# A fused matmul, GELU and matmul: the first load of b in two column halves

## The chip, the cores and the metric

The kernel runs on one core of a Trainium2 chip. The metric is the device time of one execution in microseconds, as the median of several runs; lower is better. A profile of one execution belongs to it: its span runs from the first to the last instruction and is a little shorter than the device time.

## What is computed

All inputs are float32: a is 1024 x 1024, b is 1024 x 2048, c is 2048 x 1024.

```python
h = np.matmul(a, b)
h = 0.5 * h * (1 + np.tanh(np.sqrt(2 / np.pi) * (h + 0.044715 * h ** 3)))
return np.matmul(h, c).astype(np.float32)
```

## The kernel before

The kernel keeps everything on the chip between the two products. It makes aᵀ in bf16 (`aT`), multiplies with b to get the transposed hidden matrix, applies GELU into `hT`, and multiplies with c. The order of all instructions is written out by hand (a manual schedule), so each engine runs its instructions in the order of the program text, and a wait at the head of an engine's order holds up everything behind it.

The columns of b are handled in stages. The first 512 columns (four tiles of 128, t = 0 to 3) are multiplied in the plain way while the inputs still arrive; this is the stage of the change. The next 512 and then the last 1024 columns, and the whole second product, go through `seven`, which computes a 2 x 2 block product with seven block multiplications instead of eight (Winograd's form of Strassen's method), with sums of blocks made on VectorE (DVE), and copies on ScalarE (ACT).

**The first loads.** a and the first 512 columns of b come over SyncE's queue (SP) as float32 into staging tiles, `sta` and `stb`. One load of a, `load_a(h, q)` (L70), brings 512 rows (half h) and 256 columns (quarter q) in runs of 1 KB. One load of b, `load_b(q)` (L74), brings two slabs of 128 rows (k = 2q and 2q+1) and 512 columns, in runs of 2 KB. Each is 512 KB. They are issued in the order a(0,0), b(0), a(1,0), then for q = 1 to 3: a(0,q), b(q), a(1,q). All other loads (the rest of b, and c) go over GpSimd's queue (POOL) and are cast to bf16 on the way; they start only when the copy into `gate` (L84) has seen a(1,2) land.

**The first stage.** `stir` (L116) runs matmuls on a tile of zeros, to warm up TensorE; they are part of TensorE's fixed order and wait for no load. `cast_a` (L99 on ACT, L101 on DVE) turns a staged quarter of a into bf16 (`ab`), `turn` transposes it on TensorE in two groups of four (L132) with a DVE copy from the accumulator bank into `aT` after each group (L133). `cast_b` (L139, on ACT) turns one slab of b into bf16 (`b1`), `block` and `mm1` (L105) are the matmuls. The beginning of TensorE's order is: four warm-ups of 256 columns; a group of transposes of a(0,0); a warm-up of 256; the second group; a warm-up of 128; then

```python
    cast_b(0, 2)
    cast_b(1)
    ab = cast_a(1, 0, nc.vector, nc.scalar)
    block(0, range(4), (0,))
    block(0, range(2), (1,))
    tn = turn(1, 0, 7, ab)
    next(tn)
```

`cast_b(0, 2)` casts slab 0 in two instructions of 256 columns each: the first holds the columns that tiles t = 0 and 1 need, the second those of t = 2 and 3. `cast_b(1)` casts slab 1 in one instruction of 512. The matmuls of `block` follow, four with slab 0 and two with slab 1, and then the transposes of a(1,0), whose cast is shared between DVE and ACT.

**The stores.** In the second product `done2` stores a finished tile of the output over SyncE's queue (`store`, L436). For the upper left block, (i, l) = (0, 0), each of the tiles j = 0, 1 and 2 is stored in two halves of 256 columns; other tiles go out in one store of 512 columns. The buffers that they are stored from (`o`) are four in rotation. The tile j = 3 of that block is computed last of all, in two halves (L380 to L383).

Of the kernel before, what the change touches and what calls it, by code (L numbers as in the profile page):

```python
# [19 lines left out]
def kernel(ctx, tc, a, b, c, out):  # L20
    nc = tc.nc
# [3 lines left out]
    H = 512  # L25
# [4 lines left out]
    bv = b.rearrange("(kt p) n -> p kt n", p=128)  # L30
# [9 lines left out]
    def slot(tag, shape, dt, name):  # L40
        return big.tile(shape, dt, name=name, tag=tag)
# [4 lines left out]
    def pieces(tag, bufs, shape, dt, name):  # L46
        return small.tile(shape, dt, name=name, tag=tag, bufs=bufs)
# [18 lines left out]
    stb = slot("x0", [128, KT, H], F32, "stb")  # L66
    sta = [slot(f"x{i}", [128, 2, 2, 4, 256], F32, "sta") for i in (1, 3)]

    def load_a(h, q):
        nc.sync.dma_start(out=sta[q // 2][:, h, q % 2],  # L70
                          in_=av[:, 4 * h:4 * h + 4, ds(q * 256, 256)])

    def load_b(q):
        nc.sync.dma_start(out=stb[:, 2 * q:2 * q + 2], in_=bv[:, 2 * q:2 * q + 2, 0:H])  # L74

    load_a(0, 0)
    load_b(0)
    load_a(1, 0)
    for q in range(1, 4):
        load_a(0, q)  # L80
        load_b(q)
        load_a(1, q)
# [7 lines left out]
    for n in range(2):  # L90
        for k in range(0, KT, 4):
            nc.gpsimd.dma_start(out=b2[:, k:k + 4, ts(n, H)],
                                in_=bv[:, k:k + 4, ds(1024 + n * H, H)])
# [341 lines left out]
    def store(mt, q0, w, ot, eng=None):  # L435
        (eng or nc.sync).dma_start(out=out[ts(mt, 128), ds(q0, w)], in_=ot)  # L436

    def done2(i, l, j, p):
        if (i, l) == (1, 0):
            ot = pieces("o", 4, [128, H], F32, "ot")  # L440
            nc.vector.tensor_copy(ot, p)
            p = ot
        n = 2 if (i, l) == (0, 0) else 1
        for q in range(n):
            r = ds(q * (H // n), H // n)
            store(4 * i + j, l * H + q * (H // n), H // n, p[:, r])

    def between2(n):
# [12 lines left out]
        elif n == "P73":  # L461
            two.t4(two.t[1], 4)

    seven(two, done2, between2)


# [28 lines left out]
```

## Time and profile before

The time before is 118.21 us, the median of three runs (118.2 to 118.34). The profiled execution had a span of 116.2 us and a mean granted TensorE clock of 0.999.

| | busy us | share of the span |
|---|---|---|
| TensorE matmul (PE) | 111.7 | 96% |
| TensorE weight load (PEld) | 76.9 | 66% |
| VectorE (DVE) | 90.3 | 78% |
| ScalarE (ACT) | 59.3 | 51% |
| GpSimd (POOL) | 11.0 | 9% |

| SyncE's loads and stores | count | KB each | median us from issue to landing |
|---|---|---|---|
| a into `sta` | 8 | 512 | 8.4 |
| b into `stb` | 4 | 512 | 8.0 |
| output, whole tiles | 12 | 256 | 2.1 |
| output, halves | 8 | 128 | 2.0 |

How to read the profile: PE and PEld are the two sides of TensorE, whose weight loads run beside the matmuls. Matmuls are pipelined, so the records of neighbours overlap, and a busy PE need not be PE at its peak; the spacing of starts tells the pace. L74 means line 74 of the kernel. "idle before, releaser" names what ended an engine's idle time. The chain of work is followed back from the last instruction: at each step to what released it. A DMA instruction's own record covers its issue on the engine's queue only; the transfer is seen in the DMA views and in what waits for it.

### The profile page before, as it was taken

The numbers are of one execution on the slowest core, as the hardware profiler recorded it, in microseconds if no ns is written. First come the engines' busy times: TensorE is split into PE (matmuls) and PEld (weight loads), VectorE is DVE, ScalarE is ACT, GpSimd is POOL, SyncE is SP. The second block draws the span as 40 slices with busy tenths as digits, with TensorE's granted clock in tenths as the row PEclk, the third lists the DMA queues.
The fourth block names the chain that finished last, engine by engine and source line by source line (L and its number), as shares of the span: only waits on it lengthen the run. The fifth ranks groups of instructions, "written<-read, shape, count | busy, mean of one in ns | idle before, by whom it ended". The sixth has DMA issues, their size and how long they took to land.

```text
span 116.2 us, 1478 instructions
## 1 busy us (share of the span) xinstructions
PE 111.7 (96%) x540; PEld 76.9 (66%) x540; DVE 90.3 (78%) x107; ACT 59.3 (51%) x99; POOL 11.0 (9%) x21
## 2 busy tenths in 40 slices
PE   5999999999999999999999999999999999999980
PEld 4655555545777447888885444588888888888860
DVE  0336666889998999844699999999999986954770
ACT  5067668989269998066699329600034982000000
POOL 2000049623322000000000000000000000000000
PEclk9999999999999999999999999999999999999999
DMA  2999999999999999998000000070000002014993
GB/s 83 298 356 393 395 395 321 206 206 206 206 208 213 211 213 211 213 209 164 4 0 0 0 6 0 7 264 0 0 0 0 0 0 96 0 69 171 370 364 109
DMA packets 13542, 17.91 MB, mean 154 GB/s; under 512 B 736, under 2 KB 8928, under 8 KB 13536
## 3 DMA queue, kind: packets, MB, share of 16 engines
q0 software_dynamic: 5344, 7.34, 35.6%
q1 hardware_dynamic: 8192, 10.49, 25.2%
q8 instruction: 4, 0.07, 0.2%
q14 instruction: 2, 0.02, 0.0%
HBM read 20.97 MB, written 4.19 MB: 217 GB/s over the span
## 4 chain that ended last, share of the span: by engine, by line
PE 96%; DVE 1%; issue 0%
PE ps L197 76%; PE ps L105 12%; PE ps L116 4%; PE pt L132 4%; DVE aT L133 0%; DVE ot L382 0%; DVE warm L50 0%
## 5 line engine op out<-in xcount | busy, mean ns | idle before, releaser
L197 PE MATMUL ps<-x,s 128*128 128x512 f32 x128 | 29.6, 391 | 0.0
L197 PEld LDWEIGHTS ps<-x,s 128*128 128x128 f32 x128 | 24.0, 188 | 5.1
L197 PE MATMUL ps<-x,x 128*128 128x512 f32 x96 | 22.9, 394 | 0.0
L197 PEld LDWEIGHTS ps<-x,x 128*128 128x128 f32 x96 | 18.0, 188 | 3.9
L105 PE MATMUL ps<-aT,b 128*128 128x512 bf16 x64 | 16.3, 379 | 0.0
L305 ACT ACTIVATE v<-ps 128x512 f32<-128x512 f32 x10 | 6.0, 598 | 19.4 <-PE ps L197 19.4
L197 PE MATMUL ps<-c_sb,hT 128*128 128x512 bf16 (+1 forms) x72 | 14.2, 356 | 0.0
L197 PE MATMUL ps<-x 128*128 128x512 f32 x56 | 13.2, 393 | 0.0
L197 PEld LDWEIGHTS ps<-x 128*128 128x128 f32 x56 | 10.2, 188 | 2.7 <-ACT u L305 0.4
L133 DVE COPY aT<-pt 128x512 bf16<-128x512 bf16 x16 | 6.8, 424 | 6.4 <-PE pt L132 6.4
L197 PEld LDWEIGHTS <-hT 128*128 128x128 bf16 x72 | 6.9, 98 | 7.0 <-issue 0.5
L109 ACT ACTIVATE hT<-ot 128x512 bf16<-128x512 f32 x18 | 10.5, 625 | 1.5 <-DVE ot L310 1.3
L310 DVE TENSOR_TENSOR ot<-ps,v 128x512 f32<-128x512 f32 x10 | 6.7, 688 | 5.2 <-DMA out_dram<-ot 3.8
L197 PE MATMUL ps<-aT,b 128*128 128x512 bf16 x48 | 10.7, 379 | 0.0
L310 DVE TENSOR_TENSOR ot<-ps,u 128x512 f32<-128x512 f32 x10 | 6.7, 689 | 5.1 <-ACT u L305 5.1
L155 DVE TENSOR_TENSOR x<-c_sb 128x1024 fp32r<-128x1024 bf16 x8 | 9.2, 1221 | 0.0
L132 PEld LDWEIGHTS <-ab 128*128 128x128 bf16 x64 | 4.9, 102 | 5.5 <-DVE ab L101 1.9
L197 PEld LDWEIGHTS <-b 128*128 128x128 bf16 x48 | 4.6, 97 | 5.7 <-issue 0.3
L105 PEld LDWEIGHTS <-b 128*128 128x128 bf16 x64 | 5.5, 98 | 4.1 <-ACT b L139 0.5
L99 ACT ACTIVATE ab<-sta 128x512 bf16<-128x512 f32 x10 | 6.0, 625 | 3.3 <-DMA sta<-in_a_dram 3.3
L305 ACT ACTIVATE u<-ps 128x512 f32<-128x512 f32 x10 | 5.8, 596 | 3.4 <-PE ps L197 3.2
L109 ACT ACTIVATE hT<-ps 128x512 bf16<-128x512 f32 x14 | 7.3, 596 | 0.4 <-PE ps L105 0.3
(39 smaller groups left out, 115.6 us busy)
## 6 DMA issues: line engine op xcount, KB each, us to landing
sta<-in_a_dram SPq DMA_DIRECT2D x8, 512.0 KB, 8.4
c_sb<-in_c_dram POOLq DMA_DIRECT2D x8, 512.0 KB, 19.9
b<-in_b_dram POOLq DMA_DIRECT2D x6, 512.0 KB, 11.5
out_dram<-ot SPq DMA_DIRECT2D x12, 256.0 KB, 2.1
stb<-in_b_dram SPq DMA_DIRECT2D x4, 512.0 KB, 8.0
out_dram<-ot SPq DMA_DIRECT2D x8, 128.0 KB, 2.0
```

The source lines that it names most:

```text
L99: nc.scalar.activation(dst, src, AF.Copy)
L105: nc.tensor.matmul(p, b1[:, k, ts(t, 128)], aT[:, h, k], start=(k == 0), stop=(k == KT - 1))
L109: nc.scalar.activation(hT[h][:, t], p, AF.Gelu_apprx_tanh)
L116: nc.tensor.matmul(ps[0, 3][:, 0:w], warm[:, 0:128], warm[:, 0:w], start=True, stop=True, skip_group_check=True)
L132: nc.tensor.transpose(pt[:, n, ts(m, 128)], ab[:, m, ts(n, 128)], ident)
L133: nc.vector.tensor_copy(aT[:, h, 2 * q + n], pt[:, n])
L155: nc.vector.tensor_tensor(out=dst[:, r], in0=x[:, r], in1=y[:, r], op=op)
L197: nc.tensor.matmul(p[:, ds(c0, w)], l[:, k, ts(j, 128)], r[:, k, ds(c0, w)], start=(start and k == 0), stop=(k == self.kt - 1), skip_group ...
L305: nc.scalar.activation(st, p, AF.Copy)
L310: nc.vector.tensor_tensor(out=ot, in0=p, in1=st, op=ADD)
```

## The change

b's first load is split by columns: `load_b(0, 2)` issues one load for columns 0 to 255 of slabs 0 and 1 and one for columns 256 to 511, each of 256 KB and in runs of 1 KB. The other three loads of b stay whole. It is for the first half-cast of `cast_b(0, 2)`, which then waits for the first of the two loads instead of the whole. The second half-cast waits for the second one.

With the second edit the tile j = 2 of the upper left output block is stored whole instead of in two halves. SyncE's queue then carries 13 loads and 19 stores instead of 12 and 20, and the stores behind that tile keep their number in the queue's order.

```diff
-    def load_b(q):
-        nc.sync.dma_start(out=stb[:, 2 * q:2 * q + 2], in_=bv[:, 2 * q:2 * q + 2, 0:H])
+    def load_b(q, n=1):
+        for i in range(n):
+            r = ds(i * (H // n), H // n)
+            nc.sync.dma_start(out=stb[:, 2 * q:2 * q + 2, r], in_=bv[:, 2 * q:2 * q + 2, r])
 
     load_a(0, 0)
-    load_b(0)
+    load_b(0, 2)
     load_a(1, 0)
...
-        n = 2 if (i, l) == (0, 0) else 1
+        n = 2 if (i, l) == (0, 0) and j < 2 else 1
         for q in range(n):
             r = ds(q * (H // n), H // n)
             store(4 * i + j, l * H + q * (H // n), H // n, p[:, r])
```

## The prediction

> **What bounds the kernel now.** I read the page first: the engines, and the chain that ended last.
>
> ```profile
> PE   111.7 (96%) x540; PEld 76.9 (66%) x540; DVE 90.3 (78%) x107; ACT 59.3 (51%) x99; POOL 11.0 (9%) x21
> ...
> PE 96%; DVE 1%; issue 0%
> ```
>
> TensorE carries 96% of the chain; busy time alone would not prove a bound, but the chain says that almost every step was released by the one before it on the same engine. Then the chain in order of time, at the place where b's first load is used (start, length, what):
>
> ```profile
> 1.19 3.78 PE ps L116 x8
> 4.97 0.01 issue
> 4.99 0.61 PE pt L132 x4
> 5.59 0.96 PE ps L116 x2
> 6.55 0.35 PE pt L132 x4
> 6.90 0.28 PE ps L116 x2
> 7.18 1.32 PE ps L105 x6
> 8.50 0.35 PE pt L132 x4
> 8.85 0.02 issue
> 8.88 0.44 DVE aT L133
> ```
>
> From 1.19 to 8.85 us TensorE runs without a hole: the warm-up matmuls of `stir` (L116), eight transposes (L132), then the first six matmuls that need b (L105). The warm-ups stand in TensorE's own order and wait for no load. After this there is one DVE step of 0.44 us and then TensorE to 112.98 us. The timeline of the same stretch (start, length, engine, line, what, idle before and its releaser) shows who waits for which load:
>
> ```profile
> 6.56 1.24 ACT L139 ACTIVATE b<-stb 128x256 bf16<-128x256 f32 x3 [4.33 <-DMA stb<-in_b_dram]
> ...
> 7.03 1.47 PE L105 MATMUL ps<-aT,b 128*128 128x512 bf16 x6
> ...
> 7.33 0.24 PEld L105 LDWEIGHTS <-b 128*128 128x128 bf16 x2 [0.19 <-ACT b L139]
> ...
> 7.86 0.15 PEld L105 LDWEIGHTS <-b 128*128 128x128 bf16 x2 [0.28 <-ACT b L139]
> ...
> 7.96 0.43 DVE L101 CAST ab<-sta 128x512 bf16<-128x512 f32 x1 [0.59 <-DMA sta<-in_a_dram]
> ...
> 8.44 0.23 PEld L132 LDWEIGHTS <-ab 128*128 128x128 bf16 x4 [0.43 <-DVE ab L101]
> ```
>
> ACT idles 4.33 us for b's first load; that looks like the prize. But the six matmuls take 1.47 us, that is five spacings and a last one of 0.38: (1.47 - 0.38) / 5 = 0.218 us each. Elsewhere three take 0.81 us: (0.81 - 0.38) / 2 = 0.215. So the weight loads that waited 0.19 and 0.28 us for ACT cost the matmuls about 5 x 0.003 = 0.015 us. The next thing does cost: six matmuls at 0.217 from 7.03 are issued by 8.33, and the transposes start only at 8.44, when DVE's cast of the second a load (7.96 to 8.39) is done. The **second load of a**, `load_a(1, 0)`, is what binds, by 0.11 us, and it stands in the queue right behind the load that is changed.
>
> Last, the windows of the DMA (start:end, length, five engines' busy time, clock, DMA share, GB/s):
>
> ```profile
> 4.00:4.50 0.50, 0.50 (x3) 0.25 (x1) 0.26 (x1) 0.00 (x0) 0.00 (x0) 1.00 0.99 262
> 4.50:5.00 0.50, 0.48 (x3) 0.02 (x2) 0.43 (x1) 0.00 (x0) 0.00 (x0) 1.00 0.86 184
> ...
> 9.00:9.50 0.50, 0.41 (x5) 0.14 (x3) 0.30 (x1) 0.06 (x1) 0.00 (x0) 1.00 1.05 410
> 10.50:11.00 0.50, 0.50 (x6) 0.27 (x4) 0.50 (x2) 0.46 (x2) 0.00 (x0) 1.00 1.08 383
> ```
>
> By adding up the bytes of all such windows I can say which load is moving: 0.52 MB (the first a load) are through at 3.65 us, 1.05 MB (plus b's first) at 5.6. So the first two lines are b's first load, with the DMA engines 86 to 99% busy and yet slow; the third is b's second load, in the same 2 KB runs and fast; the fourth is a, in 1 KB runs.
>
> **What the Trainium skill says.** "DMA: Bandwidth & Descriptors", section "Queues, rings and completion order": each DMA engine takes one queue's descriptors in ring order, and a load is split over the 16 engines. So the order of issue on SyncE is the order of landing; the trace agrees (landings used at 4.24, 6.56, 7.96, 9.44 us in the order of issue). The same page, "Why small descriptors are slow (HBM only)": each packet has an overhead of some 3 beats of 32 bytes, so 1 KB is 35 beats for 32 and 2 KB 67 for 64; an estimate from this is 4.5% less rate at 1 KB. The trace has 383 (1 KB) against 410 and 397 GB/s (2 KB; the 397 is the window from 13.0 to 13.5 us), 5%; I use the trace.
>
> **The change part by part.**
>
> *First half earlier.* b's first 256 columns (0.26 MB) are through when 0.79 MB are: by the windows at 4.45 us, and with the lag of about 0.6 to 0.9 us between bytes and use (3.65 to 4.24 for a, 5.6 to 6.56 for b) ACT can cast them near 5.3 instead of 6.56. The second half-cast still waits for the whole half megabyte, so it starts near 6.6 to 6.65 where it started at 6.88, and the cast of k=1 ends near 7.7 instead of 7.80. Queued behind them on ACT is half of the second a cast, which waits for its own load at 7.96 anyway. What TensorE gets is the 0.015 us above: it reaches its first b matmul at 7.03 because of the warm-ups. **Worth: 0 to 0.015 us, and the latter vanishes in the 0.11 us wait behind it.**
>
> *1 KB runs.* At a's rate the 0.524 MB take 0.524/0.383 = 1.369 us; at 404 GB/s (the mean of 410 and 397, the windows of b's second load and its third) they take 1.298: **+0.07 us**. The second load adds one completion packet per engine; at most one 1 KB packet's 0.04 us, I take 0.02. Together the next load is **0.09 us** later.
>
> *One more issue on SyncE.* About 0.5 us each at the start (1.23 to 1.73). The issue of `load_a(1, 0)` moves from 1.78 to about 2.25. Its bytes begin to move at 5.6 us, so this costs 0; the work that hides it is the queue of earlier bytes. Behind it all later issues move by at most 0.5 us, with some four loads in the queue ahead: 0.
>
> *Stores.* For one tile (j=2) two stores of 128 KB become one of 256 KB at 75 to 77 us. The DMA is otherwise idle there (28% share from 72 to 80), SyncE has no other work, and the next writer of such a buffer comes at 94.4: 0.
>
> *Sum.* The second a load, binding by 0.11 us, is used at 7.96 + 0.09 = 8.05, and every step behind it moves by as much: DVE's cast, the transposes, and, as all later loads are 0.09 later too, the next rounds, which have no room (at 12.03 and 16.07 ACT waits for the DMA while DVE has just come free). TensorE's chain has no slack from 8.44 to 112.98 to take it up. 118.21 + 0.09 = **118.3 us**, 0.08% more, which can't be told from no change.
>
> **The rivals.** *Slow start grows* (slower). From 4.0 to 5.0 us 109 packets of 2 KB took (0.99 + 0.86) x 0.5 x 16 = 14.8 us of engine time, 0.136 each, against 0.084 in the window from 9.0 (1.05 x 8 / 100). Some 180 packets were that slow: 180 x 0.052 / 16 = 0.6 us lost. I don't know why. If the loss is per packet, twice as many packets lose it twice: +0.6 on the +0.09, **118.9 us**. For it: the engines are busy, not starved, in that stretch. Against: b's first 70 packets ran at 404 GB/s with the same runs, and so did its second load.
>
> *Slow start eases* (a little faster). "DMA: Bandwidth & Descriptors", "Latency and other measured facts", tells of streams in lock-step that fall on the same memory channels (its pitches are far larger than the 8 KB here, and it calls the mechanism an inference). All 16 engines end the first a load within 0.5 us, so they start b in step; other runs may break that. Then the second a load comes up to 0.6 us sooner, but TensorE can use only 0.11 of it before its own matmuls bind at 8.33; afterwards DVE, which casts the third a pair right after a copy that ends at 12.04, sets the pace. **118.1 us** at best. For a gain over 0.24 us I find no idle time on TensorE that this change could reach.
>
> **How the numbers follow.** The plain sum 0.47 (118.3), slow start grows 0.29 (118.9), eases 0.24 (118.1). The first gives "within 0.2%" (118.0 to 118.45) nearly always, the second slower, the third mostly within, with a part faster because a bound of 0.11 read from one trace may be short. Faster 0.13, same 0.57, slower 0.30. The range runs from 117.95, a little under the best that I can work out, to 118.9, the full loss; the chance outside it is that a rival is larger than worked out.
>
> **What would show it.** In the new profile: the first half-cast near 5.3 with an idle time of some 3 us, the first L105 matmul still at 7.03, the cast at 7.96 moved to about 8.05 and the transposes at 8.44 to 8.5. If those transposes stand at 8.35 the start eased; at 9 it grew. It would be wrong if the first b matmul itself moves, for then the warm-ups don't set it, or if the times differ while the transposes stand still.

## The result, and the profile after

The changed kernel takes 119.58 us, the median of six runs (118.87 to 119.96), against 118.23 (118.2 to 118.43) for the kernel before beside it. The ratio is 1.0104, with a 95% interval of 1.0068 to 1.014: slower; the medians differ by 1.35 us. The kernel before repeats within 0.23 us here, the changed one within 1.1; but in the larger batches of the experiments the kernel before has outliers too (118.04 to 119.26 in 23 executions), so the spread by itself proves nothing. Five executions in the experiments (one each in runs 2, 3, 4, 7 and 18) were over 1.5% above the fastest of their kernel and are left out of the ratios; the profiles of runs 2 and 4 are of such executions. The profiled execution of the changed kernel is one of the two slowest of the six, with a span of 118.2 us where the one before had 116.2, so the sizes read from it are at the upper end.

First the chain that ended last, in order of time (start, length, what), in the changed kernel:

```profile
2.29 7.66 DMA sta<-in_a_dram
9.94 0.02 issue
9.97 0.44 DVE ab L103
10.41 0.05 issue
10.45 0.41 PE pt L134 x4
...
114.96 0.42 DVE ot L384
```

Before, TensorE's warm-ups, transposes and matmuls made up this part of the chain. Now one line stands in their place: the second load of a, issued at 2.29 and landed at 9.94. The transposes that it releases start at 10.45 where they started at 8.44, and the last step starts at 114.96 where it started at 113.00. The 2.0 us are there at the first of these points, and nothing later gives them back or adds to them.

The timeline of the same stretch (start, length, engine, line, what, idle before and releaser):

```profile
4.88 0.42 ACT L141 ACTIVATE b<-stb 128x256 bf16<-128x256 f32 x1 [2.65 <-DMA stb<-in_b_dram]
...
6.96 0.59 PE L107 MATMUL ps<-aT,b 128*128 128x512 bf16 x2
...
8.62 0.93 ACT L141 ACTIVATE b<-stb 128x256 bf16<-128x256 f32 x2 [3.32 <-DMA stb<-in_b_dram]
9.09 0.11 PEld L107 LDWEIGHTS <-b 128*128 128x128 bf16 x2 [2.03 <-ACT b L141]
9.09 1.12 PE L107 MATMUL ps<-aT,b 128*128 128x512 bf16 x4 [1.54 <-ACT b L141]
...
9.97 0.43 DVE L103 CAST ab<-sta 128x512 bf16<-128x512 f32 x1 [2.67 <-DMA sta<-in_a_dram]
```

The first half of b does what it was split for: its cast starts at 4.88, 1.68 us sooner. In this execution TensorE has no use for it, for its first b matmul stands behind the warm-ups, at 6.96. The second half, which the third and fourth matmuls need, is cast at 8.62 where it was 6.88, and TensorE stands idle for 1.54 us. Its granted clock stayed full from 6.59 us to the end of the work, and the mean granted clock is 0.996 or more in all six, so the loss is not a lower clock.

The windows of the DMA (start:end, length, five engines' busy time, clock, DMA share, GB/s) show the two halves and what follows:

```profile
3.50:4.00 0.50, 0.50 (x3) 0.41 (x2) 0.00 (x0) 0.00 (x0) 0.00 (x0) 1.00 1.10 387
4.00:4.50 0.50, 0.50 (x3) 0.25 (x1) 0.30 (x1) 0.00 (x0) 0.00 (x0) 1.00 1.20 301
4.50:5.00 0.50, 0.50 (x3) 0.05 (x2) 0.40 (x1) 0.12 (x1) 0.00 (x0) 1.00 0.62 143
5.00:5.50 0.50, 0.50 (x5) 0.50 (x6) 0.00 (x0) 0.30 (x1) 0.00 (x0) 1.00 0.70 158
5.50:6.00 0.50, 0.50 (x3) 0.41 (x3) 0.40 (x1) 0.00 (x0) 0.00 (x0) 1.00 0.77 170
```

The kernel before had 262 and 184 GB/s from 4.0 to 5.0 us, at shares of 0.99 and 0.86. Now the share falls to between 0.62 and 0.77: a good part of the DMA engines has nothing in flight, though the second half had been issued at 1.78 to 2.24 and the second a load from 2.29. That is one part of the loss. The other is that what is in flight moves slowly: at a share of 1.10 the engines moved 387 GB/s, so a share of 0.62 should move 218 and moved 143. The packets in the trace say how: of the 230 packets of 1 KB that start between 4.5 and 6.0 us the median takes 46 ns, but 20 take over 150 ns, up to 755, and these 20 hold 6.7 us of the 24 us that 16 engines have in this stretch. What they wait for no view shows.

The trace also holds the 16 times at which a DMA engine finished its part of a load, without the engine's number. A load counts as landed when the last one has. First and last, in us from the start:

```
                  a(0,0)       b(0), or its halves         a(1,0)
kernel before     3.87-4.21    5.58-6.54                   7.09-7.93
changed kernel    3.85-4.18    4.54-4.86  5.34-8.60        7.23-9.94
```

The first part of a(1,0) is done 0.14 us later than before, the last 2.01. In the first half the engines ended within 0.32 us of each other; in the second they come apart by 3.3 us, and the kernel waits for the last.

### The profile page after: what moved, and what is told of

Read it like the earlier page. It is cut to its first block, busy times and chain, and to the rows that moved or that the text cites. A ratio compares the mean times of both kernels' runs of the same rounds, so it can differ in the third digit from the quotient of the medians.

```text
span 118.2 us, 1472 instructions
## 1 busy us (share of the span) xinstructions
PE 111.6 (94%) x534; PEld 76.8 (65%) x540; DVE 90.2 (76%) x107; ACT 59.4 (50%) x99; POOL 11.0 (9%) x21
## 4 chain that ended last, share of the span: by engine, by line
PE 88%; DMA 6%; SPq 1%; DVE 1%; issue 1%
PE ps L199 74%; PE ps L107 10%; DMA sta<-in_a_dram 6%; PE pt L134 3%; SPq L76 1%; DVE ab L103 0%; SPq L70 0%; DVE aT L135 0%; DVE ot L384 0%
## 5 line engine op out<-in xcount | busy, mean ns | idle before, releaser
L141 ACT ACTIVATE b<-stb 128x512 bf16<-128x512 f32 (+1 forms) x9 | 4.8, 575 | 6.1 <-DMA stb<-in_b_dram 6.0
```

Source lines behind the costliest of these rows:

```text
L141: nc.scalar.activation(b1[:, k, r], stb[:, k, r], AF.Copy)
```

## The experiments

Each kernel is an edit of one of the two, and each comparison is with the kernel before on the same chip. In the measured lines "b" and "a(1,0)" are first and last engine as above; they come from one profiled execution each, the ratios from all that count. The edits are cut to the lines that matter.

**1. The load's split without the store's edit.**

```diff
-        n = 2 if (i, l) == (0, 0) and j < 2 else 1
+        n = 2 if (i, l) == (0, 0) else 1
```

> The split of b's first load alone; the stores as in the kernel before. In the changed kernel the two halves are fully landed at 4.86 and 8.60 us where the whole load landed at 6.54, and the second load of a at 9.94 where it was 7.93. All theories say that this comes from the load: about 119.6 us, TensorE's fifth b-tile wait of 1.5 us there again. If the stores had a part, this run is nearer to 118.2.

Measured: 119.95 us, ratio 1.0135 (1.0093 to 1.0177); halves 4.41-5.16 and 5.37-7.29, a(1,0) 7.53-8.79. The loss is there without the store's edit; the two intervals overlap, so that edit has no part that can be told.

**2. Two loads, but cut by slab, with 2 KB runs.**

```diff
+            w = 2 // n
+            r = slice(2 * q + i * w, 2 * q + i * w + w)
+            nc.sync.dma_start(out=stb[:, r], in_=bv[:, r, 0:H])
```

> b's first load also comes as two loads of 256 KB, but cut by slab (k = 0, k = 1), so both keep runs of 2 KB; stores as in the changed kernel. Theory R (the 1 KB runs of b, taken by all engines in step, are what is slow): 118.2 to 118.4 us, second a load landed by 8.1. Theory N (a second load in the opening burst of SyncE's issues is what is slow): about 119.6, second a load landed near 10.

Measured: 119.49 us, ratio 1.0086 (1.005 to 1.0122); b 4.90-6.46 and 5.54-8.66, a(1,0) 7.85-10.03. The interval overlaps that of the cut by columns, so theory R, short runs, doesn't explain this one. The landings are of the longest execution, 121.57 us, in which the first half was late as well, and are not used for sizes.

**3. One load with 1 KB runs.**

```diff
+        if q == 0:
+            o = o.rearrange("p k (n c) -> p (k n) c", n=2)
+            i = bv[:, 0:4, 0:256]
```

> One load of 512 KB for b's first, as before, but in 512 runs of 1 KB: it reads columns 0 to 255 of slabs 0 to 3 in place of columns 0 to 511 of slabs 0 and 1, so that part of the computation works on other numbers; sizes, waits and the stores are those of the kernel before. Theory R: 119 us or more, second a load landed at 9 or later. Theory N: 118.3 (the 0.07 us of shorter runs).

Measured: 118.2 us, ratio 0.9999 (0.9983 to 1.0015); b 5.24-5.68, a(1,0) 6.79-7.92. Twice as many packets in one load cost nothing. The windows from 4 us on:

```profile
4.00:4.50 0.50, 0.50 (x3) 0.24 (x1) 0.12 (x1) 0.00 (x0) 0.00 (x0) 1.00 1.09 389
4.50:5.00 0.50, 0.47 (x2) 0.00 (x0) 0.50 (x1) 0.00 (x0) 0.00 (x0) 1.00 1.05 373
5.00:5.50 0.50, 0.36 (x4) 0.37 (x5) 0.08 (x1) 0.00 (x0) 0.00 (x0) 1.00 0.77 236
5.50:6.00 0.50, 0.50 (x4) 0.48 (x2) 0.22 (x1) 0.30 (x1) 0.00 (x0) 1.00 0.94 281
```

b's load runs at full rate, which it did not in the kernel before, and the dip comes only afterwards, when the third load begins. So 1 KB runs are not the cause, and a whole load of them is even faster at this place than one of 2 KB runs.

**4. The second a load ahead of b.**

```diff
-    load_b(0)
     load_a(1, 0)
+    load_b(0)
```

> Kernel before with the issue order a(0,0), a(1,0), b(0) in place of a(0,0), b(0), a(1,0). It asks whether the slow stretch of the DMA (184 to 289 GB/s from 4 to 6 us in the kernel before) belongs to the time or to b's load. Theory T (the time): a(1,0), in flight from 3.7, is slow, 200 to 290 GB/s from 4 to 6, and b's first is fast. Theory R: a(1,0) runs at 385 and b's first load, from 5.1 us, is slow. b can be used only when its load has landed, near 7.5 (T or R), so TensorE starts on it some 0.6 us later and the time is 118.6 to 119.

Measured: 122.34 us, ratio 1.03 (1.0234 to 1.0366); a(1,0) 5.15-5.60, b, now third, 7.10-9.57. a(1,0) ran at 385 to 391 GB/s up to 4.5 us, so the slow stretch doesn't belong to the time: theory T falls. b was far slower than theory R said, and in third place slower than it had been in second; the time is far above the 118.6 to 119 that I expected. TensorE then sat idle for 3.3 us and came back at half its pace, with starts 0.40 to 0.43 us apart where 0.22 is usual: the granted clock was 0.50 from 8.84 to 15.67 us in this execution. That is why the time lost more than the landing.

**5 and 6. Later issues held back until the first a load has landed,** in the kernel before and in the changed one.

```diff
     load_a(1, 0)
+    nc.gpsimd.tensor_copy(sta[0][:, 0, 1, 0, 0:1], sta[0][:, 0, 0, 0, 0:1])
```

> Kernel before, with SyncE's issues paced: a one-column copy on GpSimd reads the first a load and writes into the destination of a(0,1), so SyncE issues that load and all later ones only when the first a load has landed (4.2 us) instead of from 2.3 us; three loads are queued until then. The column is overwritten by the load. Theory B (the slow stretch comes from the long run-ahead of issues in the opening): b's first load moves at 380 to 410 GB/s, lands near 5.5 instead of 6.54, the second a load near 7.0, and the time is 118.1 (0.1 us less, as TensorE's own order binds next). Theory M (memory or engine side, whatever is queued): slow stretch as before, second a load near 7.9, 118.2.

> The changed kernel with the same pacing (a(0,1) and later loads issued only after the first a load has landed). Theory B: the second half of b lands near 5.6 and the second a load near 7.1 instead of 8.60 and 9.94, the time 118.1 to 118.2. Theory M: again about 119.6, halves landing up to 3 us apart.

Measured: 120.34 us, ratio 1.0146 (1.0084 to 1.0208), and 120.23, 1.0174 (1.0139 to 1.0209). With the hold a(1,0) landed sooner in both (7.53 for 7.93; 8.48 for 9.94), but a(0,1), issued at 5.15 and 5.00, finished only at 8.46-10.73 and 8.79-10.58: the engines ran dry. In the kernel before so edited the issue of a(0,1) was over at 5.51, and yet from 6.5 to 7.5 us, as engines came free from a(1,0), the DMA share was 0.83 and 0.84, with 211 and 195 GB/s. Theory B is not confirmed, and the test was blunt, since it made a new hole. It shows that a load issued a full microsecond earlier can still leave engines without packets.

**7. b's first load taken from a.**

```diff
+        src = av if q == 0 else bv
+        nc.sync.dma_start(out=stb[:, 2 * q:2 * q + 2], in_=src[:, 2 * q:2 * q + 2, 0:H])
```

> Kernel before, but the first load into b's staging tile reads from a (row pitch 4 KB) in place of b (row pitch 8 KB), with the same 256 runs of 2 KB and the same waits; so part of the computation works on other numbers. Theory P (where b's rows lie in memory makes its first load slow): the load runs at 380 to 410 GB/s and lands near 5.5; 118.1. Theories B and M without P: slow stretch as before, landing near 6.5; 118.2.

Measured: 118.11 us, ratio 0.9986 (0.9967 to 1.0004); b's place 5.99-6.56, with 238 and 217 GB/s from 4 to 5 us. The slow stretch of the kernel before is there with rows of a too: theory P falls.

**8 and 9. Issues spaced by fills on GpSimd, about one per us,** in the kernel before and in the changed one. The later loads of b have a fill of `stb` ahead of them in the same way.

```diff
+    def paced_a(h, q):
+        nc.gpsimd.memset(sta[q // 2][:, h, q % 2], 0.0)
+        load_a(h, q)
```

> Kernel before; from the third load on, GpSimd first fills the destination of each load with zeros (about 1 us each, one after the other), and SyncE's load waits for it. So the loads are issued about one per us instead of one per half us, with no wait for data. The fills are overwritten. Theory B (issues that come in a burst are delivered to the DMA engines late and in pieces): b's first load lands near 5.5 instead of 6.54, the second a load near 7, all windows from 4 us on above 340 GB/s, time 118.1. Theory M (the slow stretch comes from the memory or the engines at a change of load): as before, 6.5, 7.9, 118.2.

> The changed kernel with the same spacing of issues from its fourth load on. Theory B: second half of b near 5.6, second a load near 7, 118.1 to 118.2. Theory M: halves of b landing up to 3 us apart, second a load near 9 to 10, 119.6.

Measured: 118.76 us, ratio 1.0041 (1.0026 to 1.0056), and 119.84, 1.0124 (1.0065 to 1.0183); b 5.28-6.69 and, with the split, 4.57-5.65 and 5.49-8.41; a(1,0) 7.42-8.05 and 7.74-9.81. Theory B falls: with the issues behind the halves spaced, the second half still lands at 8.41. The fills cost something of their own: beside them DVE's cast of a(1,0) took 1.19 us in the kernel before so edited where it had taken 0.43, so the two ratios are not the loads' alone.

**10 and 11. Another load of b split:** the second (fifth in the queue), and the last (eleventh).

```diff
-    load_b(0, 2)
+    load_b(0)
...
-        load_b(q)
+        load_b(q, 2 if q == 1 else 1)
```

> The changed kernel, but the load of b that is split is the second one (fifth in the queue) and the first stays whole. Theory B: one more issue in the opening burst, but behind b's first load and the second a load; those land as in the kernel before or a little later, time 118.2 to 118.8. A theory in which only the place right behind the first a load matters: 118.2 to 118.3.

> The changed kernel, but the split load of b is the last one (eleventh in the queue)[...]. Both theories: the split costs only its shorter runs, 118.2 to 118.3. If it costs about a microsecond here as well, the cost is in the split load itself and not in the opening.

Measured: 118.16 us, ratio 0.9986 (0.9972 to 1.0), and 118.25, 0.9996 (0.9987 to 1.0004). Free, in both places; a(1,0) landed at 7.91 and 8.11. Both kernels have the store's edit, so that is free too. Neither the split as such nor its 256 more packets costs anything that can be told, and an extra load that is issued as early as 3.41 us, fifth and sixth in the queue, doesn't either. The place of the split does.

**12. The same bytes as run 3, in two loads.** The second half comes from columns 0 to 255 of slabs 2 and 3.

```diff
+            c = ds(0, H // n) if q == 0 else r
+            k0 = 2 * q + (2 * i if q == 0 else 0)
+            nc.sync.dma_start(out=stb[:, 2 * q:2 * q + 2, r], in_=bv[:, k0:k0 + 2, c])
```

> The changed kernel, with the second half of b's first load taken from columns 0 to 255 of slabs 2 and 3 in place of columns 256 to 511 of slabs 0 and 1 (part of the computation works on other numbers). These are exactly the bytes, runs and order of the run with one load of 512 runs of 1 KB, which cost nothing (118.2), but in two loads. If the boundary between two loads is what stalls the DMA engines: 119.3 or more, halves landing 2 to 3 us apart. If the addresses are (columns 256 to 511, which no load before it has read): 118.2 to 118.4, no stall.

Measured: 118.59 us, ratio 1.0036 (1.0016 to 1.0057); halves 4.40-5.94 and 5.10-7.53, a(1,0) 7.24-8.93. Its windows beside those of run 3:

```profile
4.50:5.00 0.50, 0.14 (x1) 0.00 (x1) 0.45 (x1) 0.00 (x0) 0.00 (x0) 1.00 1.52 254
5.00:5.50 0.50, 0.50 (x5) 0.48 (x6) 0.06 (x1) 0.00 (x0) 0.00 (x0) 1.00 0.61 123
5.50:6.00 0.50, 0.47 (x4) 0.18 (x3) 0.36 (x1) 0.04 (x1) 0.00 (x0) 1.00 0.68 182
```

Where one load ran at 373 GB/s, two ran at 254, and 236 became 123. The bytes, the runs and their order are those of run 3, so the boundary costs here; but the times, 117.99 to 119.57 over 20 runs, are between the two expectations, and the interval stays below that of the changed kernel (1.0068 to 1.014). So where the second half is read from, or the chip that the run fell on, has a part in the size of the loss; which it is wasn't tested.

**13. The second half behind the second a load.**

```diff
-    load_b(0, 2)
+    load_b(0, 2, 0)
     load_a(1, 0)
+    load_b(0, 2, 1)
```

The third argument, added to `load_b`, picks the half.

> The changed kernel with the issue order a(0,0), first half of b, a(1,0), second half of b. If the third load in the queue stalls whatever it is, the second a load is slow now (landed after 8); if it is the second half of b itself, the second a load runs at 380 GB/s and lands near 6.3, and the second half behind it is slow. Time: TensorE's third b matmul needs the second half; with it landed near 7.1 118.2, with a stall 119 or more.

Measured: 120.06 us, ratio 1.0175 (1.0114 to 1.0235); first half 4.65-5.08, a(1,0) 6.20-7.32, second half 7.18-8.84. Both were slow: a(1,0), third, at 234 and 274 GB/s from 4.5 to 5.5 us, and the half behind it, fourth, at 207 to 252 from 6 to 8. So neither branch of the expectation holds alone: it isn't only the third load, and not only the half.

**14. b's first load issued first of all.**

```diff
-    load_a(0, 0)
     load_b(0)
+    load_a(0, 0)
```

> Kernel before with b's first load issued ahead of a's first, so order b(0), a(0,0), a(1,0). If the addresses of columns 256 to 511 or runs of 2 KB are slow on their first touch, b's load is slow although it is first (landed after 5). If it is the place in the queue, b's load lands near 4.2 and a later load stalls. TensorE's first transposes wait for a(0,0), now landed near 5.6 or later: 119 to 120 in both cases; the views of the DMA decide, not the time.

Measured: 121.37 us, ratio 1.0282 (1.0239 to 1.0324); b 4.49-5.35, a(0,0) 5.86-6.83, a(1,0) 7.21-8.19. Windows:

```profile
2.50:3.00 0.50, 0.50 (x2) 0.38 (x2) 0.00 (x0) 0.00 (x0) 0.00 (x0) 1.00 1.09 213
3.00:3.50 0.50, 0.50 (x3) 0.36 (x2) 0.00 (x0) 0.00 (x0) 0.00 (x0) 1.00 1.08 176
...
5.00:5.50 0.50, 0.00 (x0) 0.00 (x0) 0.00 (x0) 0.13 (x1) 0.00 (x0) 1.00 1.06 373
```

The whole load with 2 KB runs is slow with nothing ahead of it, at shares of 1.08: busy engines, long packets. That is one of the two parts of the changed kernel's loss without the other, the idle engines, and it went away for the loads behind. Beside the late a(0,0), the granted clock has a part in the time: it was 0.50 from 8.66 to 12.07 us.

**15 and 16. Run 3 from the other columns, and the changed kernel with the first half's columns read twice.**

```diff
-            i = bv[:, 0:4, 0:256]
+            i = bv[:, 0:4, 256:512]
```

```diff
+            c = ds(0, H // n) if q == 0 else r
+            nc.sync.dma_start(out=stb[:, 2 * q:2 * q + 2, r], in_=bv[:, 2 * q:2 * q + 2, c])
```

> The run with b's first as one load of 512 runs of 1 KB, which moved at 377 to 389 GB/s, but from columns 256 to 511 of slabs 0 to 3 in place of columns 0 to 255 (part of the computation works on other numbers). If the stall belongs to the columns 256 to 511, in whatever cut they are first read: the load runs at 150 to 300 GB/s, lands after 6.4 and the time is 118.2 to 119. If it belongs to runs of 2 KB or to the boundary of two loads: as that run, landed near 5.7, 118.2.

> The changed kernel, but the second half of b's first load reads columns 0 to 255 of slabs 0 and 1 again, the same bytes as the first half (part of the computation works on other numbers). Sizes, number and order of the loads are those of the changed kernel. If the columns 256 to 511 stall: no stall here at the second half, landed near 5.7, and 118.2 to 118.6. If two short loads in a row stall: 119.3 or more, second half landed after 7.2.

Measured: 118.13 us, ratio 0.9992 (0.9974 to 1.0011), b 5.43-5.82, a(1,0) 6.80-7.38; and 118.85, 1.005 (1.0017 to 1.0084), halves 4.38-5.14 and 5.52-7.49, a(1,0) 7.32-8.90. The upper columns are not the cause: one load from them is fast, two loads that never touch them stall. The second time lies between the two that were expected, and its interval overlaps both run 12's and the changed kernel's. Run 15's own executions go down to 117.51 us, and that one is the profiled one: a(1,0) landed at 7.38 in it and its transposes started at 8.02, 0.42 us sooner than in the kernel before.

**17. The second half on ScalarE's queue.**

```diff
     nc.scalar.activation(g, warm[:, 0:1], AF.Gelu_apprx_tanh)
+    nc.scalar.dma_start(out=stb[:, 0:2, 256:512], in_=bv[:, 0:2, 256:512])
```

> The split kept, but the second half of b's first load is issued on ScalarE's queue (after its table load, near 2.2 us) in place of SyncE's; SyncE then has 12 loads and the stores of the kernel before. Theory Q (the descriptors of what stands third in SyncE's queue do not reach all DMA engines before 5 to 6 us, so too few bytes ahead of it leave engines idle): the other queue fills the hole, the second half lands by 5.7, the second a load by 8, time 118.1 to 118.3. Theory S (two short loads in a row stall, on whichever queue): 119 or more.

Measured: 118.71 us, ratio 1.0036 (1.0022 to 1.005); the second half 4.70-6.12, the first, still on SyncE's queue, 5.99-6.75, a(1,0) 7.43-8.26, a(0,0) 3.85-4.77. The queue started it at 1.18, sooner than I had said, so its packets share the engines with a(0,0), which lands 0.5 us later than before. Even so most of the split's loss is gone, though not all that theory Q promised: it said 118.1 to 118.3 and a second half by 5.7. The engines had a slack stretch here too (182 GB/s at a share of 0.67 from 5.0 to 5.5 us).

**18. One tiny load in second place.** 128 runs of 64 bytes, 8 KB, into a tile that nothing reads; b's load stays whole.

```diff
+    nc.sync.dma_start(out=room, in_=bv[:, 0, 0:16])
     load_b(0)
     load_a(1, 0)
```

> Kernel before with one tiny extra load (128 runs of 64 bytes, into a tile that nothing reads) between the first a load and b's first, which stays whole. Theory Q: b's first load is now third and its descriptors come late: engines idle from about 3.7 us, b's first landed after 7.5, second a load after 9, time 119.3 or more. Theory S: one short load, and whole ones behind it: 118.3 to 118.6.

Measured: 122.37 us, ratio 1.0327 (1.0282 to 1.0372); the tiny load 3.99-4.50, b 5.67-8.63, a(1,0) 7.68-9.98. From the windows and the timeline:

```profile
4.50:5.00 0.50, 0.47 (x2) 0.00 (x0) 0.50 (x1) 0.00 (x0) 0.00 (x0) 1.00 0.73 152
5.00:5.50 0.50, 0.40 (x4) 0.40 (x5) 0.05 (x1) 0.00 (x0) 0.00 (x0) 1.00 0.59 152
...
10.00:10.50 0.50, 0.50 (x3) 0.19 (x2) 0.43 (x1) 0.50 (x1) 0.00 (x0) 0.50 1.04 387
```

```profile
9.12 2.25 PE L106 MATMUL ps<-aT,b 128*128 128x512 bf16 x6 [2.10 <-ACT b L140]
```

A load of 8 KB, in front of an untouched one, gives the picture of the changed kernel: engines idle at a share of 0.59, and 3 us between the first and the last one. Twelve of the 16 engines have their part of b by 6.91, four only at 8.34 to 8.63. The tiny load's own packets are not what takes the time: its 128 took 11 ns each, which is 0.09 us per engine. The end is later than the landing explains, as in run 4. TensorE, idle for 2.10 us, does the next six matmuls in 2.25 us where they took 1.47, because the granted clock (third number from the end of a window) was 0.50 from 9.66 to 13.07 us. The last step starts at 116.47 where it was 113.00: 2.1 of these 3.5 us are b's landing, and the remaining 1.4 are all there by 13.8 us, when the clock has just come back.

## Why the prediction was wrong

**The first half.** Expected near 5.3, found at 4.88. Right in kind, and sooner than worked out: in the changed kernel the first half moved in 1 KB runs at nearly full rate (387 GB/s up to 4.0 us), while I had taken the kernel before's slow rate for it.

**No use for it.** Right for these two traces: the first b matmul stands at 6.96 (7.03 before), behind the warm-ups. But that time belongs to the trace and not to the kernel. The full clock was granted from 6.69 and 6.59 us in these two, and from between 4.16 and 7.35 in the others; in runs 1, 6, 12 and 16, with the full clock from 5.4 or sooner and the first half landed, the first b matmul stood at 6.44 to 6.59. In runs 7 and 10, with the full clock as early but b's first load whole and landed at 6.56, it stood at 7.05. So there the early half did start TensorE sooner, and the end waited for a(1,0) all the same. "Perfetto Trace Analysis" in the Trainium skill, section "DMA Optimizations", says that splitting loads may let some start sooner, and that where the DMA engines are generally idle the whole task may end sooner. The trace shows the first part of it, a cast at 4.88 in place of 6.56; but the engines were busy here, and the work was not what the end waited for.

**What binds.** Right: a(1,0) is what the end waits for, and its landing passes into the end one for one. 2.01 us of landing became 2.01 at the transposes and 1.96 at the last step. The loads still landed in the order of their issue (4.18, 4.86, 8.60 and 9.94 us); the section on queues that the prediction names makes that no general rule, and the traces show it for these loads.

**1 KB runs, +0.07, and one more set of completions, 0.02.** Nothing speaks against them, but they are too small to be told: with a split further back the ratio is 0.9986 and 0.9996, and with a whole load in 1 KB runs at this very place 0.9999 and 0.9992.

**Stores, 0.** Right: runs 10 and 11 have the store's edit and cost nothing.

**"One more issue on SyncE ... this costs 0; the work that hides it is the queue of earlier bytes."** This is the step that failed. I counted bytes and took it that what has been issued is there when an engine wants it. The second half was issued by 2.24 and wanted at 4.4; from 4.5 to 6.0 us the DMA share was 0.62 to 0.77, and the half's last part landed at 8.60. The term put at 0 was 2.0 us in the profile and 1.35 in the median. Run 18 measures it with next to nothing else changed: an 8 KB load in that place holds up b's last engine by 2.1 us (8.63 for 6.54) and a(1,0) by 2.05. That the split's shorter runs and its packets cost little was right; the 0 for one more load early in the queue was not. That the opening of the queue behaves so is shown; why it does is not.

**The rival.** I gave "slow start grows" 0.29 and 118.9 us. Its direction was right and its working wrong: it said that the loss is per packet and doubles with their number. Runs 3 and 15 have twice the packets and no loss. My reading of the windows, busy engines with long packets, was true of the kernel before; in the changed kernel there are long packets and idle engines beside them. "Slow start eases" had 118.1 us as its best. Run 15's profiled execution, 117.51, is below that: with the full clock from 5.40 us its first b matmul stood at 6.73, so that an earlier a(1,0) was worth more than the 0.11 us that I read from one trace.

**What is shown, and what is open.** Shown: the loss comes with an additional short load among the first four in SyncE's queue, with 1 KB or 2 KB runs, cut by columns or by slab; it is absent when as many packets of 1 KB come in one load, or when the split is fifth or eleventh in the queue; most of it goes when the half is put on another queue. The size varies, from 1.0036 (run 12) to 1.0135 (run 1) for a split in the same place, and not all of that is noise.

Most of it fits one sentence: the load that stands third is not with all engines before some 5 to 6.5 us, so the two ahead of it must hold enough bytes to bridge that time. In the kernel before and in runs 3 and 15 they hold 1.05 MB, enough up to about 5.0 us at full rate; in the changed kernel and runs 1, 2, 6, 9, 12, 13 and 16 they hold 0.79 MB, up to 4.4; in run 18 0.53 MB. That sentence is inferred, not measured: no view shows when a load reaches an engine.

These things don't follow from it. Whole loads in 2 KB runs are slow with busy engines wherever they stand in the opening: as the second load they land at 6.54 and 6.56 (kernel before, run 7) where whole loads in 1 KB runs land at 5.68 and 5.82, and runs 4 and 14 show it in third and first place. In run 13 the fourth load was slow as well, and in run 12 the second had its last part only at 5.94. Single packets that take many times the usual 46 ns are a good part of the changed kernel's loss, and the sentence says nothing of them. And why only three engines (in the changed kernel, at 7.31, 7.47 and 8.60) or four (in run 18) fall far behind is open.

None of the kernels beats the kernel before beyond its interval.

## What to carry to other kernels

A load that is issued is not yet moving: here one that was issued by 2.24 us had its last part at 8.60. At the opening of a queue count the loads ahead as well as their bytes, and do not put a short one among the first without measuring; if the sentence above is right, the first two must be large enough to cover the arrival of the third. Split a load further back in the queue, where it cost nothing here, or put the part on another queue, which cost 0.36% here in place of 1.04. Read a fall of the DMA share together with the rate: idle engines and slow packets are two losses. And before splitting, ask who uses the early half: here the consumer stood behind its own warm-ups, so there was next to nothing to win, and the load that did bind stood right behind the split one.

## What the runs showed of the hardware that I had not expected

- An 8 KB load in second place of the queue had a ratio of 1.0327, some 3.9 us of 118.2. In the profile 2.1 us of it are a late landing, and 1.4 came about while TensorE's granted clock was 0.50.
- The granted clock fell in steps of 3.41 us, and a wait of 2 us could be enough: with TensorE idle from 7.03 to 9.12 in run 18 it was 0.50 from 9.66 to 13.07; with TensorE idle from 6.80 in run 4 it was 0.50 from 8.84 to 15.67. After 1.54 us, in the changed kernel, it stayed full. When it first became full differed from trace to trace, from 4.16 to 7.35 us.
- Engines that come apart at the start stay apart: in the changed kernel a(1,0) finished over 2.7 us, and later loads still over 2.5, while they all run at full rate. So in this kernel the slowest engine's lag is paid by every later load.
- As the second load, 512 KB moved at 373 to 389 GB/s in 1 KB runs (run 3) and at 184 to 262 in 2 KB runs (kernel before, from 4 us on); as a later load 2 KB runs reached 410.
